# First stage of a hybrid backbone step: two modulation tiles in h's buffers, another load order, ties on the matmul queue, stores moved forward

## The chip, the cores and the metric

The kernel runs on one core of a Trainium2 chip. The metric is the device time of one execution in microseconds (us). A core has five engines that run their own instruction queues in order: TensorE (PE, matmuls and transposes), VectorE (DVE), ScalarE (ACT), GpSimd (POOL) and SyncE (SP, which here only issues DMA transfers). ACT and POOL issue some transfers too. An instruction starts when it is at the head of its engine's queue and the semaphores it names have been raised; everything behind it on that engine waits with it.

## The reference, cut to what matters

The program computes one layer for 128 context rows and 512 latent rows (640 token rows of width 1024). The change lies in what must be ready before the large input projection:

```
mod  = silu(cond) @ ada_w + ada_b          # shift1, scale1, gate1, shift2, ... (6 x 1024)
h    = x * (1 + scale1) + shift1           # cond is c_ctx for context rows, c for latent rows
proj = h @ w_in                            # q, f, i, g, hyena and gate columns

# Hyena filters, from positions alone
h = sin(freq[0]*(z @ w1 + b1)); h = sin(freq[1]*(h @ w2 + b2)); h = sin(freq[2]*(h @ w3 + b3))
h = (h @ w4) * window                      # forward and backward filter, 512 taps x 1024 channels
K = rfft(kern, 2L)                         # later y = irfft(U * K) + skip * u
```

All matmuls that need accuracy are made of three passes over a high and a low part (hi*hi, hi*lo, lo*hi), so that each operand is first split: a copy that rounds (the high part) and a subtraction (the low part).

## The kernel before, in words

One function, `start`, issues the whole first stage from a written order, the string PLAN. A token is a step and a number:

- `x` loads a token tile xs (128 rows, 512 KB) and `T` transposes it on PE, with copies into xT by ACT or DVE (L451, L458). xT lies in buffers of the tag "h": eight buffers, of which xT takes three at this time; the rest will hold the high and low parts hTh and hTl of the modulated h.
- `k` loads a third of the transform table kt and splits it into kth and ktl (`ktab`).
- `L` loads the filter's last weight w and its window win for one group of 256 channels (of four), `A` (`kern_a`, tiles ks, af, abh, abl) makes the filter taps of the group: ten matmuls ks, five products af by the window, the split abh and abl. `B` (`kern_b`, tiles kp and k) transforms them: 54 matmuls of 256 columns, whose results are the tiles ko. `W` (`kern_store`) stores ko to the scratch tensor kd, issued on ACT's queue. `mlp` is the three sine layers (tiles f and sa).
- `D` loads a column block of ada_w (2 MB, as two tiles araw of 1 MB, in three buffers), `M` multiplies it with the conditioning (two groups of matmuls ada), copies the result (md, on ACT), transposes it (adaT, on PE) and adds it up into modT on DVE. Blocks 0 and 1 are the two halves of shift1, 2 and 3 those of scale1: h 0 to 3 need blocks 0 and 2, h 4 to 7 need 1 and 3.
- `h` (`make_h`) modulates one eighth of xT and splits it into hTh and hTl. `V` (`v_unit`) is the first projection: 120 matmuls of 256 columns for each of V0 and V1, with weights raw split into wh and wl. `e` (`m1_operands`) prepares the operands m5, m7, m6, m4 of the second stage with 12 operations of DVE each. `g`, `w` and the two-digit tokens are the second stage, a fast matrix product whose matmuls write the banks ma, mb and mc; its weight tiles are rm and their splits are named wmg, wma, wmu, wms and wmv.

The scheduler of the language then moves the steps' instructions among each other within each engine. What it arrives at is fixed at build time; the engine queues run it in order. Small strings say which engine does a copy or a subtraction: HMOD for the modulation, WSUB for the low part wl of the first eight streamed weight tiles, COPIES for copies.

All loads of this stage sit in one queue, SP's. Line numbers below are those of the kernel before.

Of the kernel before, what the change touches and what calls it, by code (L numbers as in the profile page):

```python
# [17 lines left out]
P = 128  # L18
# [123 lines left out]
COPIES = {'x': 'SSVSSSSSSS', 'h': 'SSSSSSSV', 'm': 'SV', 'k': 'VSS', 'w': 'SVVS', 'v': 'VSSS', 'a': 'SSSSSSSSSVVSSSSSSSSS', 'o': 'SSSSSSSSVSSS'}  # L142
# [21 lines left out]
def body(tc, I, O):  # L164
# [15 lines left out]

    def tt(out, a, b, op, eng=None):
        return (eng or V).tensor_tensor(out=out, in0=a, in1=b, op=op)  # L182
# [23 lines left out]
    psum = {}  # L206
# [194 lines left out]
    def ada_quad(nb, i):  # L401
        raw = ada["raw"].pop((nb, i))
        if i == 0:
            ada["ps"][nb] = mm_bank(f"ada{nb}")
        ps = ada["ps"][nb]
        for g in range(4):
            PE.matmul(ps[32 * g:32 * g + 32, :], scT[:, 4 * i + g, :], raw[:, g, :], start=i == 0, stop=i == 1)
# [34 lines left out]
    se, close_se = pool("se")  # L442
    xT = Pairs([hp.tile([P, 2, T], F32, tag="h", bufs=KT, name=f"xT{i}") for i in range(3)]
# [49 lines left out]
    def filter_mlp():  # L493
# [36 lines left out]
    def kern_a(cc, loaded):  # L530
# [3 lines left out]
        tt(wsd[:, 0], w4[:, 0], w4[:, 1], ALU.add)  # L534
        tt(wsd[:, 1], w4[:, 0], w4[:, 1], ALU.subtract)
# [6 lines left out]
        for jt in range(NB):  # L542
            ps = sc_bank(f"ks{cc}_{jt}")
            PE.matmul(ps, hf_hi[:, jt * P:jt * P + P], whl, start=True, stop=False)
            PE.matmul(ps, hf_lo[:, jt * P:jt * P + P], whl, start=False, stop=True)
# [14 lines left out]
    def kern_b(cc, ab):  # L560
# [17 lines left out]
        for kt in range(2):  # L578
            pk = [o_bank(f"k{cc}_{kt}_{eo}") for eo in range(2)]
            for eo in range(2):  # L580
                for x in range(2):
                    for j2 in range(2):
                        jt = 2 * eo + j2
                        off = 256 + x * 1024 + jt * 256 + kt * P
                        for i, (a, b) in enumerate(PASSES):
                            PE.matmul(pk[eo][:, x * 256:x * 256 + 256], kth_[a][:, off:off + P], ab[b][1 + jt][:, x, :],
                                      start=i == 0 and j2 == 0, stop=i == 2 and j2 == 1)
# [12 lines left out]

    def order_after(ins, prev):
        if prev is not None:
            tc.add_manual_dep(
                ins.ins, prev.ins.name,
                mybir.DependencyInfo(mybir.DependencyClass.NoSync, mybir.DependencyReason.DATA),
                reason="issue order")
# [123 lines left out]
    def start():  # L730
# [3 lines left out]
        def step(op, i):  # L734
# [38 lines left out]

        for tok in PLAN.split():
            if tok == "mlp":
                if HP:
                    with tc.high_priority():
                        filter_mlp()
                else:
                    filter_mlp()  # L780
                continue
            step(tok[0], int(tok[1:] or 0))
# [1024 lines left out]
```

## Time and profile before

| what | value |
|---|---|
| median of 3 runs | 1413.76 us (1411.71 to 1414.21) |
| the profiled execution's own time | 1413.15 us |
| its span in the trace | 1411.4 us |
| PE busy | 1371.7 us, 97% of the span |
| DVE, ACT, POOL busy | 995.7, 620.0, 63.4 us |
| first matmul of V0; last of V1 | 70.45 us; 115.40 us |
| first matmul of the second stage (ma) | 115.52 us |

The span starts before the first instruction; 1.75 us of the execution's time lie outside it. In a timeline a row gives start, duration, engine, line, operation, output and inputs, sizes and a count, and in brackets the idle time ahead of it with what ended it. Waits are listed as engine, line, what was waited for: us in total, times, longest. A row of a table by stretches gives the busy time of PE, PEld (weight loads), DVE, ACT and POOL, then the clock that PE was granted (1.00 is full), the share in which the DMA engines were busy, and GB/s.

### The profile page before, as it was taken

What the parts mean: (1) busy time and instruction counts of PE and PEld (TensorE: products, weight loads), DVE (VectorE), ACT (ScalarE), POOL (GpSimd) and SP (SyncE); (2) the same over time, 40 slices, a digit from 0 to 9 for tenths busy, and PEclk for the clock granted to TensorE, in tenths of its full rate; (3) what the DMA queues carried; (4) which work ended last, traced back from release to release, by engine and by line L of the source; (5) the groups of instructions that cost most, each with busy time, mean ns of one, the idle gap of its engine ahead of it and who ended that gap; (6) DMA issues with size and microseconds to landing.
All of it is one profiled execution on the core that took longest, in us unless ns stands there. A gap on an engine that the chain in (4) does not pass through costs nothing. (4 is left out here: it accounts for less than half of the span.)

```text
span 1411.4 us, 23424 instructions
## 1 busy us (share of the span) xinstructions
PE 1371.7 (97%) x9513; PEld 1290.8 (91%) x9513; DVE 995.7 (71%) x1752; ACT 620.0 (44%) x1010; POOL 63.4 (4%) x56
## 2 busy tenths in 40 slices
PE   4999999999999999999999999999999999999997
PEld 2689889899999999999999999988999999998886
DVE  6886786656889743648888786568987776765426
ACT  3555554442323211536655655227654443542121
POOL 4230000010000000000000000000000000000003
PEclk9999999999999999999999999999999999999999
DMA  7944666675323373432222223551653213267211
GB/s 246 334 139 146 208 207 195 184 232 193 101 83 102 90 246 131 135 115 82 81 86 77 64 63 109 174 196 75 169 162 102 81 59 118 89 201 263 75 60 75
DMA packets 198855, 195.63 MB, mean 139 GB/s; under 512 B 7581, under 2 KB 155773, under 8 KB 197980
## 3 DMA queue, kind: packets, MB, share of 16 engines
q1 hardware_dynamic: 194860, 179.75, 40.5%
q0 software_dynamic: 2160, 9.15, 1.8%
q10 hardware_dynamic: 1728, 5.24, 0.9%
q8 instruction: 74, 1.21, 0.4%
q14 instruction: 33, 0.27, 0.1%
HBM read 162.91 MB, written 31.21 MB: 138 GB/s over the span
## 5 line engine op out<-in xcount | busy, mean ns | idle before, releaser
L182 DVE TENSOR_TENSOR wl<-raw,wh 128x1024 fp32r<-128x1024 f32 x96 | 117.3, 1223 | 133.1 <-ACT wh L358 132.3
L358 ACT CAST wh<-raw 128x1024 fp32r<-128x1024 f32 x90 | 94.1, 1049 | 220.9 <-PE pb L612 41.0
L1431 PE MATMUL fo<-wh,act 128*128 128x512 f32 (+1 forms) x440 | 130.7, 380 | 0.0
L1431 PEld LDWEIGHTS fo<-wh,act 128*128 128x128 f32 x440 | 81.2, 188 | 16.0
L1431 PE MATMUL fo<-wl,act 128*128 128x512 f32 (+1 forms) x220 | 83.4, 379 | 0.0
L612 PE MATMUL hy<-hTh,wh 128*128 128x320 f32 x256 | 79.6, 311 | 0.0
L612 PE MATMUL hy<-hTh,wl 128*128 128x320 f32 x256 | 79.1, 309 | 0.0
L612 PE MATMUL hy<-hTl,wh 128*128 128x320 f32 x256 | 79.1, 309 | 0.0
L612 PE MATMUL f<-hTh,wh 128*128 128x320 f32 x224 | 70.7, 316 | 0.0
L612 PE MATMUL f<-hTl,wh 128*128 128x320 f32 x224 | 69.7, 311 | 0.0
L612 PE MATMUL f<-hTh,wl 128*128 128x320 f32 x224 | 69.2, 309 | 0.0
L182 POOL TENSOR_TENSOR y<-y,gb 128x512 f32<-128x512 f32 x8 | 11.6, 1454 | 888.4 <-ACT y L171 888.1
L1431 PEld LDWEIGHTS fo<-wl,act 128*128 128x128 f32 x220 | 41.3, 188 | 7.9
L612 PEld LDWEIGHTS hy<-hTh,wh 128*128 128x128 f32 x256 | 48.1, 188 | 0.0
L612 PEld LDWEIGHTS hy<-hTl,wh 128*128 128x128 f32 x256 | 48.1, 188 | 0.0
L612 PEld LDWEIGHTS hy<-hTh,wl 128*128 128x128 f32 x256 | 48.0, 188 | 0.0
L171 ACT ACT_TABLE_LOAD x36 | 46.2, 1283 | 1.4 <-PEq L1791 0.7
L715 PE MATMUL v<-wl,hTh 128*128 128x256 f32 x160 | 45.0, 286 | 1.6 <-DVE wl L182 1.6
L715 PE MATMUL v<-wh,hTl 128*128 128x256 f32 x160 | 45.1, 284 | 0.1
L715 PE MATMUL v<-wh,hTh 128*128 128x256 f32 x160 | 44.9, 285 | 0.0
L612 PEld LDWEIGHTS f<-hTl,wh 128*128 128x128 f32 x224 | 42.2, 188 | 0.0
L612 PEld LDWEIGHTS f<-hTh,wh 128*128 128x128 f32 x224 | 42.1, 188 | 0.0
(2293 smaller groups left out, 4699.6 us busy)
## 6 DMA issues: line engine op xcount, KB each, us to landing
raw<-in_w_in SPq DMA_DIRECT2D x52, 512.0 KB, 3.8
araw<-in_ada_w SPq DMA_DIRECT2D x20, 1024.0 KB, 6.5
rm<-in_w_in SPq DMA_DIRECT2D x28, 512.0 KB, 4.6
rp<-in_ffn_w_in SPq DMA_DIRECT2D x24, 512.0 KB, 5.4
raw<-in_ffn_w_out SPq DMA_DIRECT2D x22, 512.0 KB, 4.6
rf<-in_ffn_w_in SPq DMA_DIRECT2D x18, 512.0 KB, 5.2
sd<-my SPq DMA_DIRECT2D x28, 320.0 KB, 2.3
kk<-kd SPq DMA_DIRECT2D x20, 256.0 KB, 2.7
```

Of the source, the lines that this page charges most:

```text
L171: r = S.activation(out, in_, func, bias=bias, scale=scale)
L182: return (eng or V).tensor_tensor(out=out, in0=a, in1=b, op=op)
L358: (V.tensor_copy if HIE[i] == "V" else S.copy)(hi, raw)
L612: r = PE.matmul(ps[:, 0:HT], w[a][:, k, :], x[b][:, k, c0:c0 + HT], start=k == 0 and i == 0, stop=k == kt - 1 and i == 2)
L715: PE.matmul(ps[:, (t - t0) * 256:(t - t0) * 256 + 256], hT[b][:, k, t * P:t * P + P], w[a][:, k % 4, :], start=k == 0 and i == 0, stop=k = ...
L1431: PE.matmul(ps, x(t, b, k0 + kk), w[a][:, kk, :], start=first and kk == 0 and i == 0, stop=last and kk == nk - 1 and i == 2)
```

## The change

- The first block of ada_w is loaded as four tiles of 512 KB into buffers of the tag "h", which are free at that time, and its loads come ahead of those of kt; the other three blocks share the three buffers as before.
- The order of PLAN is another up to the second stage. Token tiles 0 and 4 are loaded first, the table kt after the first block; the first transposes stand between the second and third sine layer; block 1 follows block 2 with nothing between; the order of h, B and M differs; A3 (the taps of the fourth group) stands behind V0, and the stores W0 to W3 stand further forward.
- Ties (issue order alone, on one engine): on PE the first matmul of block 1 comes behind the last product of group 0's transform, that of block 3 behind the last ks of group 2, the transposes of tile 0 behind the second sine layer's matmul; on ACT the splits of kt come behind a sine; on DVE the two sums wsd of group 0 come behind the second layer's clamp.
- HMOD: all modulation is on ACT (before, h 1 and h 4 were on DVE). WSUB: the eight subtractions for wl are on DVE (before, five of them on POOL). The three copies of kt are on ACT (before, one on DVE).

```diff
-PLAN = """x0 k0 L0 k1 x4 k2 p mlp t L1 T0 x3 T4 A0 x2 D0 T2 A1 x1 L2 B0 M0 T1 D2 A2 M2 T3 h0 L3 B1 D1 A3 h1 B2 M1 D3 h2 h3 M3 h4 W2 W0 h5 h6 h7 W1 q V0 e0 B3 g0 W3 V1 m w0 e2
+PLAN = """x0 x4 L0 p mlp L1 x3 T4 t D0 A0 k0 k1 k2 T3 x2 x1 T2 D2 A1 M0 T1 D1 B0 L2 M2 h0 h1 h2 h3 W0 A2 B1 M1 D3 L3 W1 B2 M3 h4 h5 h6 h7 V0 A3 W2 e0 B3 g0 V1 q W3 m w0 e2
...
-HMOD = "SVSSVSSS"
+HMOD = "SSSSSSSS"
 HSUB = "GVVVVGVG"
-WSUB = "VGGVVGGG"
+WSUB = "VVVV"
...
+            x = PE.matmul(ps[32 * g:32 * g + 32, :], scT[:, 4 * i + g, :], raw[:, g, :], start=i == 0, stop=i == 1)
+            if (i, g) == (0, 0) and nb in (1, 3):
+                order_after(x, net["k", 0] if nb == 1 else net["ks", 2])
...
+    ada_first = [hp.tile([P, 2, T], F32, tag="h", bufs=KT, name=f"araw0_{i}").rearrange("p a t -> p (a t)")[:, 0:D].rearrange(
+        "p (a n) -> p a n", a=2) for i in range(4)]
...
-    def x_transpose(t, xs):
+    def x_transpose(t, xs, after=None):
...
+        x_transpose(0, xs0, net["f2"])
...
-        cpy("k", i, kth[:, cs], raw)
+        order_after(S.copy(kth[:, cs], raw), net["sin", "31"])
...
+            if cc == 0:
+                order_after(x, net["clamp", "2"])
...
             elif op == "D":
-                for n in range(2):
-                    ada_load(i, n, se, "araw", 3)
+                if i == 0:
+                    for n in range(4):
+                        SY.dma_start(ada_first[n], ada_w.rearrange("(k p) n -> p k n", p=P)[:, 2 * n:2 * n + 2, 0:512])
+                    for n in range(2):
+                        ada["raw"][0, n] = Pairs(ada_first[2 * n:2 * n + 2])
+                else:
+                    for n in range(2):
+                        ada_load(i, n, se, "araw", 3)
```

How the queues move is seen at three places. In the rows, a tile's name is followed by its number among its kind (ks3 is of group 3, md3 of block 3) and a serial number that differs between the two programs.

On ACT, around md3, the copy of the last modulation block's sums. Before:

```order
L599 DMA kd_66<-ko1_0_648 128x1024
L418 COPY md3_861<-ada3_852 128x512
L599 DMA kd_66<-ko1_1_679 128x1024
L358 CAST wh0_919<-raw0_917 128x1024
L358 CAST wh1_925<-raw1_923 128x1024
L358 CAST wh2_931<-raw2_929 128x1024
```

And now:

```order
L192 CAST whl2_579<-whi2_577 64x512
L192 CAST whi3_994<-wsd3_991 128x512
L192 CAST whl3_996<-whi3_994 64x512
L365 CAST wh0_847<-raw0_845 128x1024
L427 COPY md3_814<-ada3_805 128x512
L365 CAST wh1_853<-raw1_851 128x1024
```

The cast of the first streamed weight tile, raw0, and two casts of group 3's filter weight stand ahead of md3 now; before, the three casts of raw stood behind it.

On PE, the ten matmuls ks3 (filter taps of group 3). Before, they stand right behind the last product of group 1:

```order
L586 MATMUL k1_1_1_652<-abh1_4_389,ktl_136 128x256
L544 MATMUL ks3_0_694<-whl3_691,hf_hi_133 128x512
L407 MATMUL ada3_852<-araw3_0_838,scT_101 32x512 x4
L545 MATMUL ks3_0_694<-whl3_691,hf_lo_134 128x512
L544 MATMUL ks3_1_705<-whl3_691,hf_hi_133 128x512
```

Now they stand behind the last matmul of V0:

```order
L725 MATMUL v0_4_964<-wh1_853,hTh3_835 128x256
L725 MATMUL v0_4_964<-wh1_853,hTl3_836 128x256
L725 MATMUL v0_4_964<-wl1_854,hTh3_835 128x256
L561 MATMUL ks3_0_999<-whl3_996,hf_hi_137 128x512
L562 MATMUL ks3_0_999<-whl3_996,hf_lo_138 128x512
```

On DVE, the products af3 with the window that follow them. They stand behind group 2's results ko2 and ahead of all that the second stage needs (57 instructions from the first af3 to wmu0l, the first u-part of its weights, the operands of `e0` and `e2` among them):

```order
L189 TENSOR_TENSOR ko2_1_802<-k2_1_1_775,ev2_1_800 128x512
L189 TENSOR_TENSOR ko2_1_802<-ev2_1_800,k2_1_1_775 128x512
L189 TENSOR_TENSOR af3_0_1002<-ks3_0_999,win3_729 128x512
L189 TENSOR_TENSOR af3_1_1013<-ks3_1_1010,win3_729 128x512
L189 TENSOR_TENSOR af3_0_1002<-af3_0_1002 1x256
L189 TENSOR_TENSOR af3_1_1013<-af3_1_1013 1x256
```

Before, the same rows stood ahead of the sums modT of block 3:

```order
L182 TENSOR_TENSOR af3_1_708<-ks3_1_705,win3_609 128x512
L182 TENSOR_TENSOR af3_0_697<-af3_0_697 1x256
L182 TENSOR_TENSOR af3_1_708<-af3_1_708 1x256
L551 SCALAR_TENSOR_TENSOR af3_0_697<-af3_0_697,skp_all_118 1x256
L551 SCALAR_TENSOR_TENSOR af3_1_708<-af3_1_708,skp_all_118 1x256
L182 TENSOR_TENSOR modT_119<-adaT3_863,prT2_112 128x8
```

SP's loads stand in this order now: constants, xs 0 and 4, w and win of groups 0 and 1, xs 3, the four tiles of block 0, kt, xs 2 and 1, blocks 2 and 1, w and win of group 2, block 3, w and win of group 3, the first three raw. Before, kt stood among the first, block 2 behind w and win of group 2, and block 1 behind those of group 3.

More of the change, by code (lines that the diff above doesn't have):

```diff
@@ L179, in act, with order_after @@
         return r
+    def order_after(ins, prev):
+        if prev is not None:
+            tc.add_manual_dep(
+                ins.ins, prev.ins.name,
+                mybir.DependencyInfo(mybir.DependencyClass.NoSync, mybir.DependencyReason.DATA),
+                reason="issue order")
     def tt(out, a, b, op, eng=None):
@@ L205, in body @@
     wp, close_wp = pool("wp")
-    psum = {}
+    psum, net = {}, {}
     def psum_open(name, tags):
@@ L457, in x_transpose @@
             for k in range(4):
-                PE.transpose(ps[:, k * P:k * P + P], xs[:, (4 * q + k) * P:(4 * q + k + 1) * P], ident)
+                x = PE.transpose(ps[:, k * P:k * P + P], xs[:, (4 * q + k) * P:(4 * q + k + 1) * P], ident)
+                if q == 0 and k == 0:
+                    order_after(x, after)
             for i in range(2):
@@ L483, in sin_layer @@
         V.scalar_tensor_tensor(a, k, MAGIC, a, ALU.subtract, ALU.subtract)
-        V.tensor_scalar(a, a, HALF, -HALF, ALU.min, ALU.max)
-        act(a, a, AF.Sin, scale=-TWO_PI)
+        net["clamp", nm] = V.tensor_scalar(a, a, HALF, -HALF, ALU.min, ALU.max)
+        net["sin", nm] = act(a, a, AF.Sin, scale=-TWO_PI)
         return a
@@ L491, in body, with filter_mlp @@
     ktl = sp.tile([P, 2304], F32R, name="ktl")
-    def filter_mlp():
+    def filter_mlp(xs0):
         ps = sc_bank("f1")
@@ L500, in filter_mlp @@
             cs = slice(hf * ORD, hf * ORD + ORD)
-            PE.matmul(ps[cs, 0:HT], w2[cs], h1[cs], start=True, stop=True)
+            net["f2"] = PE.matmul(ps[cs, 0:HT], w2[cs], h1[cs], start=True, stop=True)
         h2 = sin_layer(ps[:, 0:HT], 1, "2")
+        x_transpose(0, xs0, net["f2"])
         V.memset(hf_lo[ORD:P, :].bitcast(F32), 0.0)
@@ L533, in kern_a @@
         wsd = se.tile([P, 2, 256], F32, tag="wsd", name=f"wsd{cc}")
-        tt(wsd[:, 0], w4[:, 0], w4[:, 1], ALU.add)
-        tt(wsd[:, 1], w4[:, 0], w4[:, 1], ALU.subtract)
+        for i, op in enumerate((ALU.add, ALU.subtract)):
+            x = tt(wsd[:, i], w4[:, 0], w4[:, 1], op)
+            if cc == 0:
+                order_after(x, net["clamp", "2"])
         whi = se.tile([P, 2, 256], F32R, tag="whi", name=f"whi{cc}")
@@ L544, in kern_a @@
             PE.matmul(ps, hf_hi[:, jt * P:jt * P + P], whl, start=True, stop=False)
-            PE.matmul(ps, hf_lo[:, jt * P:jt * P + P], whl, start=False, stop=True)
+            net["ks", cc] = PE.matmul(ps, hf_lo[:, jt * P:jt * P + P], whl, start=False, stop=True)
             af = se.tile([P, 2, 256], F32, tag="af", bufs=2, name=f"af{cc}_{jt}")
@@ L599, in kern_store @@
             KQ.dma_start(kd[cc, :, f:f + n], t)
[L601 to L606, printed above, removed]
     def dense_fm(w, x, half, ps, kt=KT, after=None):
@@ L775, in start @@
             if tok == "mlp":
[L776 to L780, printed above, removed]
+                filter_mlp(xs[0])
                 continue
```

7 lines of the change are left out of this document (3 added, 4 removed).

## The prediction

> **What bounds the kernel now.** I read the page's busy times first, then who waited for whom on PE in the first 130 us, then DVE's and PE's timelines where V1 ends and the second stage begins.
>
> ```profile
> PE 1371.7 (97%) x9513; PEld 1290.8 (91%) x9513; DVE 995.7 (71%) x1752; ACT 620.0 (44%) x1010; POOL 63.4 (4%) x56
> PE f L507 <- ACT sa L171: 7.2, 1, 7.2
> PE ks L544 <- ACT abh L185: 3.1, 1, 3.1
> PE k L586 <- DVE af L182: 2.1, 1, 2.1
> PE mc L675 <- DVE wmu0l L182: 0.3, 1, 0.3
> 90.00:115.00 25.00, 25.00 (x211) 25.00 (x210) 23.26 (x37) 12.97 (x20) 0.00 (x0) 1.00 0.33 122
> 115.52 0.31 PE L675 MATMUL ma<-hTh,wmg0h 128*128 128x320 f32 x1
> 119.04 0.31 PE L675 MATMUL mc<-m5h,wmu0h 128*128 128x320 f32 x1
> 119.77 0.41 PE L675 MATMUL mc<-m5h,wmu0l 128*128 128x320 f32 x1 [0.28 <-DVE wmu0l L182]
> 118.50 1.22 DVE L182 TENSOR_TENSOR wmu0l<-rm,wmu0h 128x1024 fp32r<-128x1024 f32 x1
> ```
>
> PE is full nearly everywhere; what can be won lies in the first stage. The long waits there are in the sine layers, and two of 2 to 3 us follow. But from 90 to 115 us DVE is as full as PE (23.26 of 25.00 us), and the first product that needs prepared weights, mc, waits for DVE's wmu0l. So two chains reach 119.77 us together: PE's own work, and DVE's list up to wmu0l. Moving only one of them forward gains nothing.
>
> The other limit is SP's queue of loads; stretches of the trace, their last two columns being the busy share of the DMA engines and GB/s, and two rows of SP:
>
> ```profile
> 5.00:10.00 5.00, 2.44 (x8) 0.36 (x6) 1.98 (x6) 0.47 (x1) 4.33 (x9) 1.00 0.76 230
> 10.00:20.00 10.00, 2.88 (x12) 2.02 (x13) 5.25 (x12) 2.75 (x5) 3.63 (x3) 1.00 1.06 289
> 20.00:30.00 10.00, 6.01 (x29) 4.00 (x27) 9.95 (x26) 7.51 (x20) 3.11 (x2) 1.00 1.04 385
> 30.00:35.00 5.00, 4.26 (x15) 2.17 (x16) 4.47 (x7) 1.85 (x4) 1.15 (x1) 0.66 0.39 100
> 35.00:40.00 5.00, 5.00 (x38) 3.71 (x37) 3.21 (x10) 1.79 (x4) 0.15 (x1) 1.00 1.04 373
> 40.00:45.00 5.00, 5.00 (x44) 4.53 (x46) 4.83 (x9) 2.62 (x5) 1.80 (x1) 1.00 0.97 352
> 45.00:50.00 5.00, 4.00 (x27) 1.66 (x19) 5.00 (x9) 1.17 (x3) 2.59 (x2) 1.00 0.44 134
> 55.00:60.00 5.00, 4.79 (x40) 3.48 (x42) 4.34 (x6) 4.62 (x10) 3.13 (x2) 1.00 1.05 403
> 60.00:65.00 5.00, 5.00 (x37) 2.97 (x32) 3.19 (x9) 4.68 (x9) 2.42 (x2) 1.00 1.05 371
> 65.00:70.00 5.00, 5.00 (x35) 3.30 (x34) 4.77 (x12) 2.48 (x4) 0.18 (x1) 1.00 1.08 381
> SPq L527 <- DVE af L182: 18.5, 2, 9.3
> 33.15 0.56 SPq L527 DMA_DIRECT2D win<-in_win  x1
> ```
>
> The engines are full (share about 1) except from 30 to 35 and 45 to 50 us, where SP stood at a win whose buffer DVE's af had not yet freed, with loads of ada_w behind it. Those two holes are what the new load order removes.
>
> **The change part by part.** *Loads.* The last modulation block is needed for h 4 to 7. Before, its sums were copied at 67.89 us:
>
> ```profile
> 67.89 0.59 ACT L418 COPY md<-ada 128x512 f32<-128x512 f32 x1 [2.52 <-PE ada L407]
> 68.38 2.95 ACT L358 CAST wh<-raw 128x1024 fp32r<-128x1024 f32 x3
> 68.70 0.60 PE L431 MATMUL adaT<-cst,md 128*128 128x128 f32 x4
> 69.05 0.36 PE L586 MATMUL k<-abl,kth 128*128 128x256 f32 x1
> ```
>
> Now ACT's queue has the cast of raw0 ahead of md3, so md3 waits for raw0, which SP issues after everything else. The bytes up to and with raw0, from the tiles' sizes: constants 0.5 MB, five xs 2.6, four w 1.05, four win 2.6, kt 1.2, four blocks 8.4, raw0 0.5: 16.9; with group 0's stores (1.3), which share the engines, 18.2. By 30 us 8.1 MB had moved (5 us at 230 GB/s, 10 at 289, 10 at 385, 0.2 MB ahead); with the new order that is no less, as the queue was full there too. The remaining 10.1 MB at 376 GB/s, the mean of the five full stretches after 35 us, take 26.8 us: raw0 lands at 56.8 (55.0 at 403 GB/s, 58.7 at 352). The cast takes 1.05 us (a third of three casts, with what overlaps); md to adaT took 0.8 us and adaT to the next product 0.35. Group 1's products therefore start at 59.0. Block 3 is some 9 us earlier than before.
>
> *What stands behind that on PE.* Group 1's products were done before block 3 in the old order; now all 48 of them, group 2's 54 and V0's 120 come after adaT3, and ks3 comes after V0.
>
> ```profile
> 101.13 0.28 PE L715 MATMUL v<-wh,hTh 128*128 128x256 f32 x1
> 115.40 0.28 PE L715 MATMUL v<-wl,hTh 128*128 128x256 f32 x1
> 79.04 0.43 PE L586 MATMUL k<-abh,kth 128*128 128x256 f32 x1 [2.08 <-DVE af L182]
> 82.67 0.28 PE L715 MATMUL v<-wh,hTh 128*128 128x256 f32 x1
> ```
>
> V1's 120 matmuls start 14.27 us apart, first to last: 0.12 us each, also for the products, of the same width. So 48, 54 and 120 take 5.8, 6.5 and 14.4 us. After an idle time of 2.08 us the next 17 ran at 0.21 instead of 0.12 us, 1.6 us lost. PE has about 4 us of idle time ahead of adaT3 (block 3 itself, 1.44 MB ahead of raw0 in the queue, is 3.8 us earlier), so I add 1.6. Small waits for ACT and DVE among these products were up to a few us before; I take 1.2 (0 to 2.4). Sum: 59.0 + 5.8 + 6.5 + 14.4 + 1.6 + 1.2 = 88.5 us for the first ks3.
>
> *What stands behind ks3 on DVE.* From the first af3 to wmu0l DVE has 57 instructions, in order, of which 24 are 128x640, 4 are 128x1024, 16 are 128x512 and 13 small.
>
> ```profile
> 25.32 0.41 DVE L182 TENSOR_TENSOR af<-af 1x256 f32<-1x256 f32 x1
> 27.06 1.27 POOL L182 TENSOR_TENSOR abl<-af,abh 128x512 fp32r<-128x512 f32 x1 [5.22 <-ACT abh L185]
> 27.08 1.53 DVE L182 TENSOR_TENSOR af<-af 1x256 f32<-1x256 f32 x1
> 89.39 0.82 DVE L182 TENSOR_TENSOR mb<-hTh,hTl 128x640 f32<-128x640 f32 x1
> 90.12 0.68 DVE L182 TENSOR_TENSOR ko<-k,ev 128x512 f32<-128x512 f32 x1
> 90.72 0.67 DVE L182 TENSOR_TENSOR ko<-ev,k 128x512 f32<-128x512 f32 x1
> 100.04 1.22 DVE L182 TENSOR_TENSOR wl<-raw,wh 128x1024 fp32r<-128x1024 f32 x1
> 101.18 0.82 DVE L182 TENSOR_TENSOR m4l<-mb,m4h 128x640 fp32r<-128x640 f32 x1
> 23.26 0.73 PE L544 MATMUL ks<-whl,hf_hi 128*128 128x512 f32 x2 [1.44 <-ACT hf_hi L185]
> 24.31 0.69 DVE L182 TENSOR_TENSOR af<-ks,win 128x512 f32<-128x512 f32 x1
> ```
>
> By the distance of starts one costs 0.73, 1.14 and 0.60 us, and the small ones about 0.2 on average: 17.5 + 4.6 + 9.6 + 2.6 = 34.3 us. The first af came 1.05 us after the first ks. For waits in between I take 1.5 us (0 to 3.8): two abl of POOL, each of which can stretch a DVE row by 1.1 us (the same 1x256 sum took 1.53 us beside POOL's abl, 0.41 without), and casts of ACT. So wmu0l is done at 88.5 + 1.05 + 34.3 + 1.5 = 125.3 us. PE's own work would be through sooner: ks3, V1 and group 3 (ten matmuls of twice the width, so 2.4, then 14.4 and 6.5) bring it to ma at 111.8, and 48 matmuls of 0.147 us (24 of them took 119.04 less 115.52, 3.5 us) to 118.9. It waits 6.4 us, and 1.6 us of slow clock follow.
>
> The Trainium skill, page "SBUF — State Buffer", section "Who interferes with whom", says that a DVE tensor_tensor with both inputs in SBUF and a GpSimd instruction that reads SBUF exclude each other for a whole instruction. The pair of rows at 27.06 us agrees. By that rule the two abl in the list could cost up to 2.6 us in place of the 1.5 that I took for all waits, and the sum would be 1.1 us more.
>
> *The sum.* Before, the same work (24 more matmuls, 3.5 us, now come ahead of mc) stood at 119.77 + 3.5 = 123.3. Now it is 125.3 + 1.6 = 126.9. That is 3.6 us later, and behind it the two programs are the same but for small reorderings.
>
> *Edits at nothing.* The sine layers run some 4 us sooner, since wsd and kt no longer stand between them on DVE; the loads hide it, and without that cover it would be a gain of 4 us. Modulation on ACT: about 2 us more there, hidden while V0 works on h 0 to 3; if that cover were gone, V0 would start its second half up to 2 us later. WSUB: two wl of the first stage move to DVE (2.3 us) into time where it waits for ks3, and three later ones stand where PE waits for nothing; if not covered, 2.3 us. The split of block 0 into four loads costs SP two more issues, under 1 us, ahead of a full queue. The stores move no more bytes.
>
> **The rivals.** *PE sets the end.* If DVE's list didn't decide (its casts and sums interleave better than a queue in order lets me think), ma would start at 111.8 in place of 115.52: 3.7 us faster, 1409.4. For it: PE's 97%. Against it: 23.26 of 25 us on DVE before, with group 3's taps already done by then. *Holes in SP's queue.* The last tile of block 1 and the two of block 3 wait for buffers that ada matmuls free, and block 1's are tied behind the last product of group 0. If that came late, SP would stand as it did at 33.15 us. The load ahead keeps the engines busy until about 50 us (15.7 MB), and group 0's products ended at 44 before; from 50 on, each us late is a us at the end. Two holes like those at 30 and 45 us (276 and 242 GB/s missing over 5 us, 3.7 and 3.2 us at 376) give 3.6 + 6.9: 1423.7. *The change leaves the end where it is.* With no slow clock after either wait (3.2 us), the sum is 0.4 us: 1413.6; the tenth of DVE's work that I could have misjudged cancels as easily.
>
> **How the numbers follow.** The forecast, that DVE's list behind ks3 decides: 0.50, at 1413.15 + 3.6 = 1416.8 us by the profiled execution's own time; the median of the runs shown is 0.6 us above that execution, so 1417.4 against it; I write 1417.0. Its own range is 1412 to 1421 (waits and loads at their bounds, not all at once). PE sets the end: 0.20. Holes: 0.18. No change: 0.12. Two runs of this kernel are told apart from about 0.2%, 2.8 us. Of the forecast's 0.50 some 0.20 lie within that. So faster 0.21, within 0.2% 0.33, slower 0.46, and 1408 to 1423 holds eight in ten.
>
> **What would show it.** In the trace after: the DMA share without the two holes, and the last ada matmuls near 54 us. md3 starting only behind the cast of raw0, near 58. PE idle for some us ahead of it, then matmuls of 256 columns at 0.21 us. V0 ending near 88. DVE idle for about 10 us ahead of the first af3 and full from there; and PE idle ahead of mc for 4 to 7 us, released by wmu0l, near 125 us. I am wrong if PE doesn't wait there (then it is the first rival), if DVE's af3 starts before V0 ends, or if md3 starts ahead of 55 us.

## The result, and the profile after

The changed kernel takes 1431.09 us (median, 1430.33 to 1436.09) against 1413.99 us (1411.71 to 1414.33) of the kernel before, measured side by side: a ratio of 1.0136, 95% interval 1.0123 to 1.0149. It is slower by 17 us, where 1417.0 was predicted, with 1423 as the upper end of the range. The profiled execution took 1430.37 us, its span is 1428.3. The lines of the changed kernel have other numbers: L189 is the helper of the two-input operations (L182 before), L192 that of the copies, L414 ada, L561 and L562 ks, L590 kp, L603 k, L685 the second stage, L725 V0 and V1.

What PE waited for, in the changed kernel (us in total, times, longest):

```profile
PE ks L561 <- DVE whl L189: 7.8, 2, 4.9
PE adaT L440 <- ACT md L427: 3.2, 2, 2.5
PE kp L590 <- POOL abl L189: 2.9, 1, 2.9
PE mc L685 <- ACT wmu0h L630: 2.8, 1, 2.8
PE ma L685 <- DVE wmg1l L189: 1.4, 1, 1.4
```

The waits for the sine layers are mostly gone from the top of the list. In their place stand waits for whl, md, abl and wmu0, the longest of each from 50 us on (of the 7.8 us for whl, 2.95 lie at 19 us). The timelines of its SP, PE, ACT and DVE, in order of time (start, duration, what ran, idle time ahead and what ended it; "..." marks where rows are left out):

```profile
40.58 8.98 SPq L405 DMA_DIRECT2D araw<-in_ada_w  x2
51.90 3.05 SPq L357 DMA_DIRECT2D raw<-in_w_in  x3
58.03 0.76 PE L561 MATMUL ks<-whl,hf_hi 128*128 128x512 f32 x1 [4.89 <-DVE whl L189]
...
62.57 2.42 PE L414 MATMUL ada<-araw,scT 128*32 128x512 f32 x16
64.92 0.38 PE L590 MATMUL kp<-abh,kth 128*128 128x256 f32 x1
65.06 0.59 ACT L427 COPY md<-ada 128x512 f32<-128x512 f32 x1 [0.77 <-PE ada L414]
66.11 0.36 PE L603 MATMUL k<-abh,kth 128*128 128x256 f32 x1
...
86.98 0.38 PE L725 MATMUL v<-wh,hTl 128*128 128x256 f32 x1 [2.23 <-DVE hTl L189]
98.63 0.40 PE L561 MATMUL ks<-whl,hf_hi 128*128 128x512 f32 x1
99.29 1.29 DVE L189 TENSOR_TENSOR af<-ks,win 128x512 f32<-128x512 f32 x2 [6.68 <-PE ks L562]
110.31 4.12 DVE L189 TENSOR_TENSOR mb<-hTh,hTl 128x640 f32<-128x640 f32 x4
136.65 1.04 ACT L630 CAST wmu0h<-rm 128x1024 fp32r<-128x1024 f32 x1 [2.23 <-DVE rm L189]
137.75 0.41 PE L685 MATMUL mc<-m5h,wmu0h 128*128 128x320 f32 x1 [2.80 <-ACT wmu0h L630]
137.87 1.22 DVE L189 TENSOR_TENSOR wmu0l<-rm,wmu0h 128x1024 fp32r<-128x1024 f32 x1
```

Read from the top: the two loads of block 3 were issued between 40.6 and 49.6 us, the second as its buffer came free. The ten ks2 began only at 58.03, after 4.89 us of waiting for whl2 on DVE, and all ten with it took 4.5 us, at a granted clock of 0.50, where the ten ks3 later took 2.3 us. Block 3 stood behind them, md3 behind block 3 (not behind the cast of raw0: it waited for PE's ada), and 48 of group 1's 54 products behind adaT3, at 66.1 us (its six kp stand just ahead of adaT3, at 64.92). V0's last matmul started at 98.5, DVE was idle for 6.68 us until the first af3, and its list reached wmu0l at 137.87. Before, wmu0l stood at 118.50. PE's wait of 2.80 us at mc was ended by ACT's wmu0h, and that cast by the tile rm of the same DVE list.

Stretches of the trace of the changed kernel (busy time of PE, PEld, DVE, ACT, POOL; clock; DMA share; GB/s):

```profile
30.00:35.00 5.00, 3.90 (x24) 2.08 (x21) 2.83 (x5) 2.80 (x7) 5.00 (x4) 1.00 1.04 384
45.00:50.00 5.00, 4.98 (x43) 3.33 (x41) 2.48 (x4) 4.16 (x8) 3.28 (x2) 1.00 0.56 213
55.00:60.00 5.00, 1.97 (x5) 1.61 (x6) 4.70 (x14) 1.24 (x2) 0.00 (x0) 0.50 1.02 332
90.00:100.00 10.00, 10.00 (x76) 9.76 (x76) 1.99 (x4) 3.52 (x5) 0.00 (x0) 0.95 0.21 81
130.00:140.00 10.00, 5.48 (x30) 4.87 (x30) 10.00 (x19) 5.44 (x11) 0.00 (x0) 0.94 0.42 132
```

Of the two holes in the loads one is gone (30 to 35 us: a share of 1.04 instead of 0.39), the other is still there (45 to 50 us: 0.56; before 0.44). From 90 to 100 us DVE did 1.99 us of work, before 9.58; from 130 to 140 us it was full and PE had 5.48 us.

### The profile page after: what moved, and what is told of

Its sections match the earlier page's. It is cut to its first block, busy times and chain, and to the rows that moved or that the text cites. A ratio compares the mean times of both kernels' runs of the same rounds, so it can differ in the third digit from the quotient of the medians.

```text
span 1428.3 us, 23432 instructions
## 1 busy us (share of the span) xinstructions
PE 1379.1 (97%) x9513; PEld 1296.3 (91%) x9513; DVE 998.0 (70%) x1752; ACT 622.4 (44%) x1015; POOL 51.9 (4%) x51
## 3 DMA queue, kind: packets, MB, share of 16 engines
q8 instruction: 74, 1.21, 0.3%
## 5 line engine op out<-in xcount | busy, mean ns | idle before, releaser
L189 DVE TENSOR_TENSOR wl<-raw,wh 128x1024 fp32r<-128x1024 f32 x101 | 124.1, 1232 | 138.2 <-ACT wh L365 133.0
L725 PE MATMUL v<-wh,hTl 128*128 128x256 f32 x160 | 45.9, 288 | 2.4 <-DVE hTl L189 2.2
L725 PE MATMUL v<-wl,hTh 128*128 128x256 f32 x160 | 45.8, 287 | 0.7 <-DVE wl L189 0.7
L725 PE MATMUL v<-wh,hTh 128*128 128x256 f32 x160 | 45.5, 287 | 0.0
L189 POOL TENSOR_TENSOR y<-y,gb 128x512 f32<-128x512 f32 x8 | 11.6, 1452 | 888.0 <-ACT y L171 887.7
```

What stands on the lines that cost most here:

```text
L725: PE.matmul(ps[:, (t - t0) * 256:(t - t0) * 256 + 256], hT[b][:, k, t * P:t * P + P], w[a][:, k % 4, :], start=k == 0 and i == 0, stop=k = ...
```

## The experiments

Each kernel is the changed kernel with the edits named, unless it says "before". A kernel's ratio is to the kernel before, run on the same chip in the same set. The sets ran on different chips, and the median of the kernel before lay between 1412.2 and 1414.0 us in them; differences of some 2 us between medians of different sets are therefore within what the chips differ. The fourth column is when DVE starts wmu0l in the profiled execution, the last the span less that start.

| kernel | median us | ratio (95%) | wmu0l | span | span less wmu0l |
|---|---|---|---|---|---|
| changed | 1431.09 | 1.0136 (1.0123 to 1.0149) | 137.87 | 1428.3 | 1290.4 |
| 1 no tie of block 1 | 1429.78 | 1.0124 (1.0107 to 1.0141) | 135.18 | 1425.4 | 1290.2 |
| 2 no ties | 1428.99 | 1.0112 (1.0097 to 1.0128) | 134.72 | 1425.7 | 1291.0 |
| 3 A3 ahead of V0 | 1421.28 | 1.0063 (1.0047 to 1.0079) | 126.76 | 1418.3 | 1291.5 |
| 4 engines as before | 1432.33 | 1.0135 (1.0120 to 1.0150) | 140.88 | 1430.2 | 1289.3 |
| 5 before, with A3 behind V0 | 1417.85 | 1.0044 (1.0028 to 1.0060) | 126.54 | 1415.7 | 1289.2 |
| 6 B1 ahead of A2 | 1422.58 | 1.0070 (1.0054 to 1.0086) | 132.32 | 1422.6 | 1290.3 |
| 7 both moves (3 and 6) | 1417.66 | 1.0037 (1.0025 to 1.0049) | 125.31 | 1415.3 | 1290.0 |
| 8 A2 ahead of h, and 3 | 1418.81 | 1.0043 (1.0026 to 1.0059) | 126.44 | 1416.5 | 1290.1 |
| 9 as 7, no ties | 1417.25 | 1.0034 (1.0021 to 1.0048) | 125.59 | 1415.4 | 1289.8 |
| 10 as 7, casts late | 1414.53 | 1.0015 (1.0006 to 1.0024) | 122.39 | 1412.2 | 1289.8 |
| 11 as 10, no ties | 1417.70 | 1.0036 (1.0023 to 1.0048) | 126.70 | 1418.0 | 1291.3 |
| 12 as 7, two casts late | 1414.21 | 0.9999 (0.9990 to 1.0009) | 122.27 | 1412.8 | 1290.5 |
| 13 as 8, whl2 off DVE | 1417.81 | 1.0033 (1.0021 to 1.0046) | 125.65 | 1416.2 | 1290.6 |
| 14 as 13, two casts late | 1417.43 | 1.0033 (1.0021 to 1.0046) | 124.04 | 1413.8 | 1289.8 |
| 15 as 12, wl 1 and 2 on POOL | 1416.04 | 1.0016 (1.0007 to 1.0025) | 121.50 | 1411.4 | 1289.9 |

The last column is the main reading of the study: wmu0l starts anywhere between 121.5 and 140.9 us, and the rest of the span is 1289.2 to 1291.5 us in all of them. (In the kernel before it is 1411.4 less 118.50, 1292.9; 3.5 us of that are group 3's products that come later there, which leaves 1289.4.) Whatever an edit does to the first stage, the end moves by what it does to the start of wmu0l. This marks where the end is decided; that DVE alone decides it does not follow. PE waited for the first mc for 2.3 to 3.6 us in the changed kernel and in runs 1, 2, 4 and 5, for 0.2 to 1.8 us in runs 3, 7 to 10, 12 and 14, and not at all in runs 6 (which had waited 2.25 us for wmg1l shortly before), 11, 13 and 15. Once A3 stands ahead of V0, PE's own work and DVE's list arrive nearly together.

**Where A3 stands (runs 3 and 5).** Two edits from two sides: A3 is taken back ahead of V0 in the changed kernel, and put behind V0 in the kernel before.

```diff
 # run 3, from the changed kernel
-... B2 M3 h4 h5 h6 h7 V0 A3 W2 ...
+... B2 M3 A3 h4 h5 h6 h7 V0 W2 ...
 # run 5, from the kernel before
-... B1 D1 A3 h1 B2 ... q V0 e0 ...
+... B1 D1 h1 B2 ... q V0 A3 e0 ...
```

> The changed kernel with group 3's filter taps (step A3: ks3, and af3 and its splits behind it) moved ahead of h 4 to 7 and V0 in the order of steps; both ties stay. ks3 then stands among V0's first matmuls instead of behind its last. Theory A, 'DVE's list behind ks3 sets the end': DVE's idle time ahead of the first af3 (6.7 us behind 4.4 us in the changed kernel) is used for part of the list, PE's waits for kp3, ma and mc from 100 to 138 us (2.9, 1.4 and 2.8) and the slow clock behind them go, wmu0l comes near 130 instead of 139.1, and the time falls by 7 to 9 us, to 1422 to 1424. Rival B, 'PE is late by itself, with a clock that is slow from 50 to 65 us and its work from group 1 on': mc is not earlier by more than 2 us and the time stays within 1429 to 1432.

> The kernel before with one edit: its step A3 (ks3, af3 and the splits behind it) stands behind V0 in the order of steps, as in the changed kernel; loads, ties and engines as before. Theory A, 'the work behind ks3 on DVE sets the end wherever it is put late': V0 ends near 95 us, the first af3 comes near 96 to 97, and with the 39.8 us that the list took in the changed kernel wmu0l is done near 136 instead of 119.7; mc follows there with 3.5 us of group 3's products already done, so the time rises by 11 to 14 us, to 1424 to 1427. Rival B, 'most of the changed kernel's loss comes from its first 66 us (the late block 3, the slow clock) and not from A3's place': within 4 us of the kernel before, 1412 to 1418.

Run 3, its DVE:

```profile
79.54 0.69 DVE L189 TENSOR_TENSOR af<-ks,win 128x512 f32<-128x512 f32 x1 [0.68 <-issue]
```

A stretch of 10 us of it:

```profile
100.00:110.00 10.00, 10.00 (x86) 10.00 (x85) 9.97 (x14) 5.49 (x9) 0.00 (x0) 1.00 0.45 145
```

Run 5, its DVE:

```profile
90.12 1.29 DVE L182 TENSOR_TENSOR af<-ks,win 128x512 f32<-128x512 f32 x2
```

And what its PE waited for:

```profile
PE mc L675 <- ACT wmu0h L620: 2.3, 1, 2.3
PE ma L675 <- DVE wmg1l L182: 1.5, 1, 1.5
```

Run 3 came out as theory A had it, and somewhat more: the first af3 is 20 us earlier, DVE and PE are both full from 100 us, wmu0l is 11.1 us earlier and the time falls by 9.8 us, where 7 to 9 were expected. Run 5 shows the same mechanism in the kernel before, with the same two waits at the second stage; the list from the first af3 to the start of wmu0l takes 36.4 us there. But its price is 0.44%, 6.2 us, and not the 11 to 14 of theory A, since V0 ended near 89 us and not at 95; it lies between theory A and rival B, which had within 4 us. So A3's place by itself does not make 17 us. The changed kernel is also late in reaching V0's end, by 9 us against run 5.

**Ties and the hole in the loads (runs 1 and 2).** The first matmul of a modulation block is no longer tied.

```diff
-            if (i, g) == (0, 0) and nb in (1, 3):
+            if (i, g) == (0, 0) and nb == 3:     # run 1;  run 2: nb in ()
```

> The changed kernel with one edit: the first matmul of modulation block 1 is no longer tied behind group 0's last product (block 3's tie stays). It tells whether the hole in SP's queue decides when block 3 comes. Theory A, 'block 3 is held by ks2': the second tile of block 3 is issued near 41 us instead of 49.6, but block 3's matmuls stay behind the last ks2, and ks2 stays behind whl2 of DVE, which came at 57.9; so the copy md3 stays at 64 to 65 us (65.06 in the changed kernel) and the time at 1430 to 1432. Rival B, 'the hole holds block 3': md3 comes near 58 us, group 1's products start near 59.5 instead of 66.3, and the time falls by about 7 us, to 1424.

> The changed kernel without either tie: neither block 1 nor block 3 is tied. Block 3's matmuls now stand ahead of ks2 on PE, and md3 ahead of the cast of raw0 on ACT. Theory A, 'block 3 is held by ks2 and comes serially behind it': block 3 now runs while ks2 waits for whl2, so group 1's products start right behind the last ks2, near 62 us instead of 66.3, the first ks3 comes some 4 us earlier (94 instead of 98.2), and the time falls by 3 to 5 us, to 1426 to 1428. Theory B, 'the hole alone': 1424, as without block 1's tie. Rival C, 'these starts don't matter, since the list behind ks3 refills the gap': 1430 to 1432.

Run 1, the stretch with the hole:

```profile
45.00:50.00 5.00, 4.69 (x38) 3.52 (x36) 2.94 (x6) 4.68 (x10) 2.87 (x2) 1.00 1.05 393
```

Its PE and ACT:

```profile
55.98 0.77 PE L561 MATMUL ks<-whl,hf_hi 128*128 128x512 f32 x1 [6.29 <-DVE whl L189]
62.60 0.59 ACT L427 COPY md<-ada 128x512 f32<-128x512 f32 x1 [0.36 <-PE ada L414]
```

Run 2, its ACT, PE and DVE:

```profile
57.33 0.57 ACT L427 COPY md<-ada 128x512 f32<-128x512 f32 x1
57.64 0.77 PE L561 MATMUL ks<-whl,hf_hi 128*128 128x512 f32 x1 [2.77 <-DVE whl L189]
62.90 0.35 PE L590 MATMUL kp<-abh,kth 128*128 128x256 f32 x1
96.42 0.39 PE L561 MATMUL ks<-whl,hf_hi 128*128 128x512 f32 x1
98.73 1.28 DVE L189 TENSOR_TENSOR af<-ks,win 128x512 f32<-128x512 f32 x2
```

Run 1 fills the hole (0.56 to 1.05), so the hole is the tie's doing. But ks2 still waits for whl2, md3 is only 2.5 us earlier and the median 1.3 us lower, within the spread of the two: theory A rather than B. Run 2 brings md3 forward by 7.7 us, ahead of ks2, and still ks2 starts at 57.64, 0.4 us earlier than in the changed kernel, since it waits for whl2 as before. What is saved is block 3's place in the line: group 1's first product kp comes at 62.90 instead of 64.92, and the first ks3, behind V0, at 96.42 instead of 98.63. The first af3 is only 0.6 us earlier, because four other rows of DVE (wmg0l, two ko and a wl) stand ahead of it there. The median is 2.1 us lower, the ratio by 0.24%, 3.4 us; theory A's 3 to 5 is neither met clearly nor excluded.

So V0's end moved with group 1's start: from the first kp of group 1 to the first ks3 it is 33.7 us in the changed kernel, 33.5 in run 1 (62.45 to 95.97) and 33.5 in run 2. With the hole closed, or with both ties gone, V0's end came 2 to 3 us earlier, of the 10 by which it was later than forecast. The rival with the holes is out as the main cause.

**The edits costed at nothing (run 4).**

```diff
-HMOD = "SSSSSSSS"
+HMOD = "SVSSVSSS"
-WSUB = "VVVV"
+WSUB = "VGGVVGGG"
```

> The changed kernel with the old assignment of engines: the modulation of h 1 and h 4 on DVE again and the lower halves of the streamed weights 1, 2, 5, 6 and 7 on POOL again; all orders, loads and ties as changed. Theory A, 'these two edits are hidden': 1429 to 1433, the copy md3 at 65 and wmu0l near 139. Rival B, 'the lower halves that came to DVE lengthen its list': two of 1.14 us in the first stage, so wmu0l 2 us earlier and 1428 to 1429. Rival C, 'POOL's instructions stretch those of DVE': slower by 1 to 3 us, 1432 to 1434.

1432.33 us, a ratio of 1.0135 against 1.0136: the two edits cost and gain nothing here that the runs can tell, which is within some 2 us (theory A). The profiled execution itself is 2 us longer and its wmu0l 3.0 us later, which a small effect of rival C would give too. Whether it would hold where DVE has no idle time is the question of run 15.

**Group 1 ahead of ks2 (runs 6 and 7).**

```diff
 # run 6; run 7 has A3 moved as in run 3 too
-... W0 A2 B1 M1 D3 ...
+... W0 B1 A2 M1 D3 ...
```

> The changed kernel with group 1's products (step B1) ahead of group 2's taps (step A2) in the order of steps; A3 stays behind V0, both ties stay. PE then has 54 products to do from about 52 us, where it stood idle for 2.5 and 4.9 us, and ks2 and block 3 come behind them. Theory A, 'PE's gap from 50 to 58 us is what made group 1 and V0 late': group 1's 5.8 us go into the gap, the first ks3 comes near 93 instead of 98.2, and with the list behind it unchanged the time falls by 4 to 6 us, to 1425 to 1427. Rival B, 'the gap only moves, since ks2 and block 3 are now later, and V0 waits for h 4 to 7': V0's end and the first af3 stay within 2 us, time 1429 to 1433.

> The changed kernel with both moves: B1 ahead of A2, and A3 ahead of h 4 to 7 and V0. With A3 early alone the time was 1421.3 and PE waited only 3.5 us between 66 and 200 us. Theory A, 'what is left there is PE's gap from 50 to 58 us': the time falls by 4 to 6 us more, to 1415 to 1417, within 3 us of the kernel before. Rival B, 'what is left is DVE's list again': DVE was full from 96 to 120 us with A3 early; then it starts no earlier than its input, and the time stays at 1420 to 1422.

Run 6 fell by 8.5 us, more than theory A's 4 to 6 (in the profiled executions by 5.7). But only part of it is where theory A put it: the first af3 came at 97.01, 2.3 us earlier, and the list behind it was 3.3 us shorter. Group 1 no longer stood behind ks2 in this run, and its first kp came at 50.80, 14 us earlier; yet the first ks3 came only 2.6 us earlier, since PE then waited for md3. Run 6, its PE:

```profile
72.18 1.12 PE L440 MATMUL adaT<-cst,md 128*128 128x128 f32 x4 [4.58 <-ACT md L427]
96.02 0.39 PE L561 MATMUL ks<-whl,hf_hi 128*128 128x512 f32 x1
```

Run 7 came to 1417.66, 3.6 us below run 3 and just short of theory A. It has the same wait. Its SP, ACT and PE:

```profile
51.53 11.33 SPq L357 DMA_DIRECT2D raw<-in_w_in  x3
69.88 1.04 ACT L365 CAST wh<-raw 128x1024 fp32r<-128x1024 f32 x1 [1.79 <-DMA raw<-in_w_in]
70.83 0.58 ACT L427 COPY md<-ada 128x512 f32<-128x512 f32 x1
71.46 1.12 PE L440 MATMUL adaT<-cst,md 128*128 128x128 f32 x4 [4.74 <-ACT md L427]
```

And a stretch of 5 us:

```profile
65.00:70.00 5.00, 1.22 (x5) 0.93 (x5) 3.05 (x3) 1.39 (x3) 0.44 (x1) 0.58 0.90 293
```

Here md3 does stand behind the casts, as the prediction had it for raw0: all three of them wait for their weights to land, ACT's queue with them, and PE has 1.22 us of work in 5 us. The loads are part of it: SP issued those of raw1 and raw2 only at 61.9 and 62.3 us, after 9.7 us of waiting, where the changed kernel had all three out by 55.0. The profile puts that wait down to a store of ko; no run tests it.

**whl2 itself (runs 8, 13 and 14).** Run 8 puts A2 ahead of h 0 to 3, so that whl2 stands ahead of hTl on DVE; run 13 computes it on POOL and ACT as well.

```diff
 # run 8 (with A3 as in run 3)
-... L2 M2 h0 h1 h2 h3 W0 A2 B1 ...
+... L2 A2 M2 h0 h1 h2 h3 W0 B1 ...
 # run 13, on top of run 8
-            x = tt(wsd[:, i], w4[:, 0], w4[:, 1], op)
+            x = tt(wsd[:, i], w4[:, 0], w4[:, 1], op, G if cc == 2 else V)
-        tt(whl[ORD:P], wsd[ORD:P], f32(whi[ORD:P]), ALU.subtract)
+        tt(whl[ORD:P], wsd[ORD:P], f32(whi[ORD:P]), ALU.subtract, G if cc == 2 else V)
-COPIES = {... 'w': 'SVVS', ...}
+COPIES = {... 'w': 'SVSS', ...}
```

> The changed kernel with A3 early as before and group 2's taps (A2) ahead of the modulation of h 0 to 3, so that wsd2, whi2 and whl2 stand ahead of the lower halves hTl on DVE; B1 stays behind A2. In the changed kernel hTl stood for 1.6 and 0.7 us ahead of whl2, which PE's ks2 waited for. Theory A, 'DVE's order ahead of whl2 holds ks2, block 3 and group 1': whl2 comes 2 to 2.5 us earlier, near 55.5, md3 near 61, and the time is 2 to 3 us below that of A3 early alone, 1418 to 1419. Rival B, 'the second tile of block 3, issued at 49.6 us, holds block 3': md3 stays at 63 and the time at 1420 to 1422.

> As the run with A2 ahead of h 0 to 3 and A3 ahead of V0 (1418.8 us), but wsd2 and the lower half of whl2 are computed on POOL, and whi2 and the rest of whl2 on ACT, so that ks2 no longer waits for DVE's queue. Theory A, 'ks2's wait for whl2 and block 3 behind it made group 1 late': ks2 starts right behind block 1's transposes, near 53 us instead of 57.8, at the full clock, group 1's products near 56 to 58, md3 comes with the load of block 3's second tile near 58 to 60, and the time falls by 4 to 6 us, to 1413 to 1415. Rival B, 'the load of block 3's second tile holds group 1': md3 not before 63 us and no more than 1 us is gained, 1417.5 to 1419. Rival C, 'POOL's longer work takes it back': whl2 comes later than 53 us, or DVE's rows beside POOL's are stretched by over 1 us in sum; 1416 to 1418.

Run 8, its PE:

```profile
57.78 0.77 PE L561 MATMUL ks<-whl,hf_hi 128*128 128x512 f32 x1 [3.35 <-DVE whl L189]
62.97 0.39 PE L590 MATMUL kp<-abh,kth 128*128 128x256 f32 x1
```

Run 13, its SP and PE:

```profile
40.61 8.72 SPq L405 DMA_DIRECT2D araw<-in_ada_w  x2
53.93 0.79 PE L561 MATMUL ks<-whl,hf_hi 128*128 128x512 f32 x1 [1.04 <-POOL whl L189]
58.36 0.41 PE L590 MATMUL kp<-abh,kth 128*128 128x256 f32 x1
```

In run 8 the move did not bring whl2 forward (md3 stayed at 64.5, near rival B's 63), so its gain of 2.5 us over run 3 is not explained by what theory A named. Run 13 did: against run 8, ks2 started 3.9 us earlier and group 1's first product (kp) at 58.36 instead of 62.97 us, with the second tile of block 3 issued as late as ever. So the wait for whl2, with block 3 and group 1 in line behind it, is what made group 1 late; the load of block 3 was not. Yet the median fell by 1.0 us only against run 8, and md3 stayed at 63.5: these are the numbers of rival B, and the time is in rival C's range too, though group 1 did not wait for the load as B had it. PE then waited elsewhere (for DVE's af four times, 0.8, 0.7, 2.0 and 0.6 us), and the first af3 came at 79.18, as in run 3. Theory A's place was right, its price in time was not. With A3 behind V0, as in the changed kernel, whl2 was not moved alone in any run. Run 14, with two casts late on top, was expected at 1410 to 1413:

> As the run with whl2 off DVE, and the casts of raw1 and raw2 without their raised priority; ks3 then stands ahead of nearly all of V0, and group 3's first products among V0's. Theory A, 'DVE's list behind ks3, ks2's wait and the casts of weights are the three places of the loss, and they add up': 1410 to 1413, equal to the kernel before or faster by up to 0.2%. Rival B, 'casts moved late cost V0 what they give to group 2': no faster than the run with whl2 off DVE alone.

It came to 1417.43, no faster than run 13: its rival B.

**Casts that wait for weights (runs 9 to 12).** The casts wh and subtractions wl of the first weights have a raised priority, so the scheduler puts them early. In run 10 those of raw0 to raw2 lose it, in run 12 those of raw1 and raw2 alone; runs 9 and 11 are 7 and 10 without ties.

```diff
-        with tc.high_priority():
+        with (ExitStack() if i < 3 else tc.high_priority()):      # run 10;  run 12: i in (1, 2)
             (V.tensor_copy if HIE[i] == "V" else S.copy)(hi, raw)
```

> The changed kernel with B1 ahead of A2 and A3 ahead of h 4 to 7, and without both ties. With the ties PE waited 4.74 us for md3, which stood on ACT behind the casts of raw0, raw1 and raw2 (the last of them at 69.9 us). Now block 3's matmuls stand among group 1's last products and md3 stands ahead of the three casts. Theory A, 'md3 behind the casts is what is left': md3 near 60 us instead of 70.8, PE has V0's first half to do while group 2's splits wait for the casts, and the time falls by 3 to 4 us against the run with ties (1417.7), to 1413.5 to 1415. Rival B, 'the loads themselves are late': PE is idle until raw2 has landed all the same, 1416 to 1419.

> The changed kernel with B1 ahead of A2, A3 ahead of h 4 to 7, both ties kept, and the casts and lower halves of raw0 to raw2 without their raised priority, so that they stand behind md3, group 2's splits and h 4 to 7 on ACT, and behind group 2's and af3 0 and 1 on DVE. Theory A, 'queues of ACT and DVE that stand at a weight still on its way hold group 2 and block 3': PE's idle time from 66.5 to 71.5 us goes, group 2's 54 products run in it, and the time falls by 4 to 5 us against 1417.7, to 1412.5 to 1414, which is no slower than the kernel before. Rival B, 'V0 needs the casts at that time anyway': PE's wait moves to V0's first product on wh0 or wl0, 1416 to 1419.

> As the run before this with late casts, and without both ties too. Theory A, 'ties and casts each hold block 3': 0 to 2 us below the run with ties, 1411 to 1413, equal to the kernel before or faster by up to 0.1%. Rival B, 'the ties cost nothing once the casts are late': the same as with ties within 1 us. Rival C, 'something that this study has not named costs the rest': over 1416.

> As the run with B1 ahead of A2, A3 ahead of h 4 to 7, both ties and late casts (1414.5 us), but only the casts of raw1 and raw2 have lost their raised priority; that of raw0 keeps it and stands ahead of md3 again, as in the changed kernel. There PE stood still for 4 us between 65 and 80 us, and V0's first product on wl0 waited 1.8 us, since the casts came at 76 to 80 us although the weights had landed near 68. Theory A, 'these 4 us of PE are still on the path': V0's first half fills them, the time falls by 1 to 3 us to 1411.5 to 1413.5, equal to the kernel before. Rival B, 'DVE's list from the first af3 (74.9 us) to wmu0l (123.6 us) sets the end there': no change, 1413.5 to 1415.5. Rival C, 'md3 behind wh0 costs what the change was found to cost': md3 moves from 63.6 to 65 or later and the time rises by 1 to 3 us.

Run 10 is 3.1 us below run 7 (1414.53, half a microsecond short of theory A and still 0.15% above the kernel before), and run 12 is level with the kernel before (0.9999, 0.9990 to 1.0009). Its median is in rival B's range and its ratio is what theory A expected, so these two are not told apart. So with the load order, the ties and the engines of the change kept, and three edits to the order (A3 ahead of V0, B1 ahead of A2, two casts without their raised priority), the 17 us are back, and nothing more. The second and third are not simply undone: the kernel before has A2 ahead of B1 and all casts at the raised priority. Taking the ties away was not a gain on top: run 9 is equal to run 7 (the number of rival B) though md3 came at 60.62 instead of 70.83 us, and run 11 is 3.2 us slower than run 10 (rival C). In run 11 ks2 stands behind block 3's matmuls, group 2's first tap af2 came 1.2 us later than in run 10 (60.84 against 59.69), its products waited 1.7, 1.4 and 1.0 us for abh and abl, and the first af3 came at 78.16 instead of 74.94. (Run 11's profiled execution, 1420.17 us, was the slowest of its five.)

**The list where DVE is full (run 15).**

```diff
 # on top of run 12
-WSUB = "VVVV"
+WSUB = "VGGVVGGG"
```

> As the run with B1 ahead of A2, A3 ahead of V0 and the casts of raw1 and raw2 late (1414.2 us, wmu0l at 122.3), but with the lower halves of the streamed weights 1, 2, 5, 6 and 7 on POOL again, as in the kernel before. Theory A, 'DVE's list up to wmu0l still sets the end there': two rows of 1.14 us leave it, wmu0l starts near 120 and the time falls by 1.5 to 2.5 us, to 1412 to 1413. Rival B, 'PE's own work sets it': wmu0l earlier, time the same within 1 us. Rival C, 'POOL's subtractions of 128x1024 come late for V0 or stretch the rows of DVE beside them': 1415 to 1418.

1416.04 us, with single executions from 1413.3 to 1417.8; the profiled one is the fastest of them, and there wmu0l started 0.8 us earlier than in run 12. Theory A is not borne out. PE waited 2.2 us for POOL's hTl3, which speaks for rival C, but run 12 has such a wait of 2.3 us as well; the cause of the 1.8 us is not settled.

## Why the prediction was wrong

The chain that it named, DVE's list behind ks3, is the one that set the end in the changed kernel, and the sign was right, though slower had been given 0.46 only. Two parts of its sum were too small, and by addition they make up the whole miss. Measured against the predicted times: the first ks3 98.6 instead of 88.5 (10.1 us), and from there to the end of wmu0l (139.1) 40.5 instead of 36.8 (3.7). Added to the 1416.8 of its sum this gives 1430.6; the profiled execution took 1430.37.

- **Group 1's products at 59.0.** This is the step that failed: 66.1, so 7.1 us. The prediction took the landing of raw0 and its cast as the last thing md3 waits for. Instead ks2 waited 4.89 us for whl2, which stood on DVE behind group 0's results, group 1's taps and two hTl, and the rest followed in series on PE. The tie of block 3 "behind the last ks2" was read as an order, and nobody asked when ks2's own operand would be there. Run 13 shows that this wait, not the load of block 3, made group 1 late, and runs 1 and 2 that V0's end follows group 1's start. The cast of raw0 ahead of md3 cost nothing in the changed kernel: md3 waited for PE's ada alone. But the 7.1 us are not simply there to be won back. Where group 1 was moved (runs 6 and 7), PE waited 4.6 and 4.7 us for md3 behind the three casts, and the first ks3 of run 6 was 2.6 us earlier, not 7: the wait that the prediction had named, of md3 for weights, came behind the one that it had missed, there with loads that were issued late.
- **From there to ks3, 29.5 us.** It took 32.5. PE stood still for 3.1 us in it, where 1.2 were taken for all small waits: 2.23 us of it for hTl3, of h 6 and 7, at 86.98. The 1.6 us for the slow clock came too, but behind this wait and not behind adaT3: from 87.4 to 90.7 us most matmuls came 0.21 us apart. The slow clock ahead of adaT3, in ks2 and block 3, is in the first term. With A3 behind V0 no edit of the changed kernel brought the first ks3 forward by more than 2.7 us (run 1).
- **DVE's list, 34.3 + 1.5 us.** The instructions were counted rightly, 57. The waits in between were 1.16, 1.27 and 1.64, 4.1 us, just above the upper bound of 3.8; the first of them was for an abl of POOL that took 3.60 us. And the four mb took 4.12 instead of 3.02 us beside the other abl of POOL. The list is late because of its input: runs 3 and 5 showed that from both sides.
- **PE sets the end (0.20), no change (0.12).** Out: PE had 5.48 us of work from 130 to 140 us. Of the 4 to 7 us that PE was to wait ahead of mc, 2.80 came there, ended by wmu0h and not by wmu0l, and 1.4 at a ma ahead of it.
- **Holes (0.18).** One hole did stay, with the mechanism named (a buffer behind the tie to group 0's last product), at block 3's second tile. It was priced at 1 us at the end for each us late; run 1 closed it, the first ks3 came 2.7 us earlier and the median was 1.3 us lower.
- **Edits at nothing.** Held within some 2 us: run 4 for HMOD and WSUB together. The first ks0 came at 19.04 instead of 23.26, and this gain was hidden as expected, though behind a queue on DVE and not behind loads. The four loads of block 0 were not tested by themselves.
- **The range.** It took the bounds of each term alone. The largest term had 55.0 to 58.7 from the loads as its bounds, and no bound for a wait on another engine in front of it.

## What to carry to other kernels

When a step is tied or ordered behind another on one engine, look up when the operands of that other step are ready, on their own engines' queues; the tie passes its wait on to all that follows. A place that sets the end (here the start of wmu0l) is found quickly by running a few different orders: the time behind it stays the same to 0.2% while its start moves; which of the engines that meet there is the late one has to be read from the waits. And a cast of a weight that is still on its way holds up its engine's whole queue: letting three such casts and their subtractions come later was worth 3.1 us here (run 10 against run 7). When one wait in a line is taken away, ask what the next one is, since it may stand close behind.

## What the runs showed of the hardware

**A short idle time is enough to halve PE's clock.** Run 10, its PE around a wait of 1.80 us:

```profile
79.88 0.58 PE L725 MATMUL v<-wl,hTh 128*128 128x256 f32 x1 [1.80 <-DVE wl L189]
80.26 0.41 PE L725 MATMUL v<-wh,hTh 128*128 128x256 f32 x1
80.47 0.41 PE L725 MATMUL v<-wh,hTl 128*128 128x256 f32 x1
```

Two stretches of it, with the granted clock ahead of the last two columns:

```profile
80.00:83.00 3.00, 3.00 (x13) 2.83 (x14) 1.80 (x4) 0.96 (x2) 3.00 (x2) 0.50 0.61 174
83.00:86.00 3.00, 3.00 (x26) 2.96 (x25) 3.00 (x5) 0.62 (x1) 0.12 (x1) 0.99 0.19 47
```

For about 3 us the granted clock was 0.50 and the matmuls came 0.21 us apart instead of 0.12. In the changed kernel the ten ks2 after a gap of 4.89 us took 4.5 us instead of 2.3. The Trainium skill, page "TensorE: Matmul & The Clock Gate", section "Part 1: The HAM clock gate (the "warmup" mystery)", says that the clock halves after at least one idle window of some 3.4 us and returns after a busy one as long. The 3 us at half speed in run 10 agree; in the changed kernel the clock stayed at 0.50 from 58.0 to some 63.7 us under work, longer than that. That 1.80 us of idle time were enough, with work on either side, does not agree, and the measurement decides.

**DVE and POOL hold each other up in either direction.** The two abl of POOL behind ks3 in the changed kernel, the second of them beside the four mb of DVE shown above (110.31, 4.12 us); then, in run 4, the four mb, the row of DVE that follows them, and the abl beside it:

```profile
102.31 3.60 POOL L189 TENSOR_TENSOR abl<-af,abh 128x512 fp32r<-128x512 f32 x1 [13.28 <-ACT abh L192]
112.44 1.32 POOL L189 TENSOR_TENSOR abl<-af,abh 128x512 fp32r<-128x512 f32 x1 [6.53 <-ACT abh L192]
```

```profile
111.88 3.02 DVE L189 TENSOR_TENSOR mb<-hTh,hTl 128x640 f32<-128x640 f32 x4
114.81 0.82 DVE L189 TENSOR_TENSOR mb<-mb,mb 128x640 f32<-128x640 f32 x1
114.78 1.99 POOL L189 TENSOR_TENSOR abl<-af,abh 128x512 fp32r<-128x512 f32 x1 [7.88 <-ACT abh L192]
```

At 112.44 DVE paid: its four mb took 4.12 us against 3.02 in run 4, where no abl fell among them, and the abl took 1.32. In run 4 POOL paid: its abl took 1.99 us, and the mb beside it the usual 0.82. At 102.31 POOL paid most, 3.60 us beside two subtractions of DVE of 128x1024, which took 1.21 us each; PE's wait of 2.9 us for abl is for this one. It agrees with the rule that the prediction cites from the Trainium skill (page "SBUF — State Buffer", section "Who interferes with whom"), and shows that either engine can be the one that pays.
